# One shared set of fourteen 8 KB buffers in place of separate homes for weights and normed rows

## The chip, the cores and the metric

The kernel runs on one core of a Trainium2 chip. The metric is the device time of one execution in microseconds (us): 773.72 us is the median of three runs (773.42 to 774.41). The core's engines work side by side, each through its own list of instructions in a fixed order: PE (TensorE, matmul), DVE (VectorE), ACT (ScalarE), POOL (GpSimd) and SP (SyncE, which issues the transfers here). Semaphores hold an instruction back until what it needs is there.

## The reference, cut to what matters

```
x: (1, 256, 1024) f32;  for l in range(2):
    sh1,sc1,gt1,sh2,sc2,gt2 = split(silu(c) @ w_ada[l] + b_ada[l], 6)
    h  = rms(x, g_mix[l]) * (1 + sc1) + sh1
    qkv_a, qkv_b(3 groups), gate_a, gate_b = split(h @ w_in[l])
    y_a = gqa_attention(rope(rms(qa)), rope(rms(ka)), va) @ w_branch_a[l]     # 8 query, 2 key/value heads
    y_b = dilated_attention(3 groups x 4 heads) @ w_branch_b[l]
    x  = x + gt1 * ((sigmoid(gate_a)*y_a + sigmoid(gate_b)*y_b) @ w_out[l])
    h2 = rms(x, g_mlp[l]) * (1 + sc2) + sh2
    x  = x + gt2 * (square(relu(h2 @ w_ff1[l])) @ w_ff2[l])                   # hidden width 4096
```

256 rows are two tiles of 128 (t = 0 and 1) on the partitions.

## The kernel before

**Weights.** All weights stream from HBM once, as tiles of 128 x 1024 f32 (512 KB). A tile lands in one of six buffers `wr`, and is split for matmuls in a reduced format: ACT writes the high part (`w<-wr`, a copy that rounds), DVE the low part (`w<-wr,w`, the difference). High and low together are one tile `w2` of 8 KB in each partition. The other operand is split in the same way (`hT`, `mT`, `oa`, `r2k`), and `mm3` makes each product of three matmuls: high by high, low by high, high by low. 236 weight tiles are split so. 96 more (`w_ada`) also land in `wr`, and DVE reduces each against silu(c) in one instruction (`s2k<-wr,c_act`, called an ada below), in the gaps of other work.

**Stages of a layer.** Norm and transposes give `hT` (normed rows, transposed, scaled and shifted; high and low, 8 KB each); then the q, k and v products; attention A (four pairs) and B (two pairs of heads) in pieces between the gate matmuls `g`; the branch products `ya`, `yb`; the output product `wo`; the residual (`s2k<-ps,gtb`, `x<-x,s2k`); then the norm again and the MLP: `ff1` and `ff2`, where a first ff1 tile (f0, four weight tiles) goes by rows t. A norm is a chain over four engines: sum of squares on ACT, `ss` on DVE, a power of one column on POOL (`ss<-ss,half`), two row scalings `xn` on DVE (`s2k<-x,ss`), eight transposes on PE (`ps<-ident,s2k`, called xT), then scale and shift and both parts of `hT` on DVE. The stretches from `wo` to `ff1` and from the MLP of layer 0 to layer 1 are called handoffs below.

**What sets the order.** The program doesn't issue as it is written. `Plan` records every operation, links them by what they read and write (`links`), and lays them out with a model of the engines (`run`, from L330): each engine takes the ready operation with the earliest due time (`due`, L304). Two things there depend on how many buffers a kind of tile has. In `due` (L311 to L325), the users of a tile are due before the first use of the tile that stands as many places later among its kind as there are buffers. In `run`, `fits` (L351 to L363) holds an operation back until a buffer of its kind is free; a tile that starts out of its turn must leave room for those that were written before it. `issue` (L460) then emits the operations in that order. The tiles of kinds in `mixed` (L138, only `"b8"`) share one set of equal buffers, which the tile framework hands out.

**Homes of 8 KB before.** `w2` has four buffers, `hT` two, and `b8` (`NB8`, L40) eight. `b8` holds the attention's q and k tiles, v, `oa`, both gate tiles `G`, the table tile, `M`, both `mT`, and those weight tiles that `spare` marks (patterns `sp_x`, `sp_wo`, `sp_f`, `sp_l` in `CFG`: four of the eight of `wo`, for one). 14 in all.

Of the kernel before, what the change touches and what calls it, by code (L numbers as in the profile page):

```python
# [12 lines left out]
F32R = mybir.dt.float32r  # L13
# [6 lines left out]
P = 128  # L20
D = 1024
S = 256
# [3 lines left out]
KT = D // P  # L26
# [10 lines left out]
  seq0="u c3 w w u c4 w w u a w w w w a v w w w w a w w w w v a w w w w b v w w y y b w w v y y v".split(),  # L37
  seq1="c2 u w w c3 u w w c4 u w w c5 w w a u w w a w w v a w w a v w w b v y y b v y y".split())
WR = 6
NB8 = 8  # L40

# [452 lines left out]
def encoder(ctx: ExitStack, tc: tile.TileContext, a: dict, out: bass.AP):  # L496
# [6 lines left out]
    tl = plan.tile  # L503
# [16 lines left out]
    def f32(t):  # L520
        return t.bitcast(F32)
# [84 lines left out]
    def split_next():  # L606
        src, spare = todo.pop(0)
        i = len(todo)
        raw = tl("sbuf", [P, 1024], F32, "wr", WR, f"wr{i}")
        if spare:  # L610
            w2 = tl("sbuf", [P, 2, 1024], F32R, "b8", NB8, f"w2{i}")
        else:
            w2 = tl("sbuf", [P, 2, 1024], F32R, "w2", 4, f"w2{i}")
        sp.dma_start(raw, src)
        act.activation(w2[:, 0], raw, AF.Copy)
        dve.tensor_tensor(w2[:, 1], raw, f32(w2[:, 0]), op=ALU.subtract)
        ready.append((w2[:, 0], w2[:, 1]))

    def weights(n=None):
        while todo and len(ready) < (n or CFG["ahead"]):  # L620
            split_next()
        return ready.pop(0)
# [37 lines left out]
            yield ps  # L660

    def h_tiles(l, w):
        return [tl("sbuf", [P, KT, S], F32R, "hT", 2, f"hT{l}{w}{i}") for i in range(2)]

    def make_h(l, w, t, hT):
        v = shg[l, w]
# [15 lines left out]
    def rope_tables(l):  # L682
        tabs = tl("sbuf", [P, 2, 2, 8, HD], F32, "b8", NB8, f"tabs{l}")
        for hf in range(2):
            g = s2k(f"gain{l}{hf}")
            sp.dma_start(g, a["gains"][l, hf].partition_broadcast(P))
            gv = g.rearrange("p (s q n) -> p s q n", s=4, q=2)
            act.activation(gv[:, :, 1, :], gv[:, :, 1, :], AF.Copy, scale=8.0)
            g = g.rearrange("p (s n) -> p s n", s=8)
            for t in range(2):  # L690
                for s0, s1, o in ((0, 2, 0), (2, 8, 1)):
                    cs = cst[:, t, o, hf, :]
                    pool.tensor_tensor(
                        tabs[:, t, hf, s0:s1, :], g[:, s0:s1, :],
                        cs[:, None, :].to_broadcast([P, s1 - s0, HD]), op=ALU.mult,
                    )
        return tabs
# [62 lines left out]
    def attention_tiles(l):  # L760
        T = {}

        z = [tl("sbuf", [P, 2, 4, S], F32, "b8", NB8, f"qk{l}{i}") for i in range(2)]
        T["qa"] = z[0][:, 0]
        T["b", 0], T["b", 1], T["b", 2] = z[0][:, 1], z[1][:, 0], z[1][:, 1]
        T["ka"] = tl("sbuf", [P, 1, S], F32, "ka", 1, f"ka{l}")
        v = tl("sbuf", [P, 2, 16, HD], F32, "b8", NB8, f"v{l}")
        T["va"] = [v[:, t, 12:14] for t in range(2)]
        T["vb"] = [v[:, t, 0:12] for t in range(2)]
        oa = tl("sbuf", [P, 2, 4, S], F32R, "b8", NB8, f"oa{l}")  # L770
        T["oa"] = (oa[:, 0], oa[:, 1])
# [172 lines left out]
    def gates(l, hT, G, u, bank):  # L944
        if u % 4 == 0:
            G.append(tl("sbuf", [P, 2048], F32, "b8", NB8, f"G{l}{u}"))
        ps = bank(f"g{l}_{u}")
# [38 lines left out]
    def mixer(l, hT, T):  # L986
# [51 lines left out]
        for t in range(2):  # L1038
            ps = [pb(f"wo{l}_{t}_{c}") for c in range(2)]

            def one(kk, c):
                lh, ll = (z[:, kk, t * P : (t + 1) * P] for z in mT)
                wh, wl = (z[:, c * 512 : (c + 1) * 512] for z in ws[kk])
                mm3(ps[c], lh, ll, wh, wl, kk == 0, kk == KT - 1)

            if t == 0:
                for kk in range(KT):
                    ws.append(weights())
                    for c in range(2):
                        one(kk, c)  # L1050
            else:
                for c in range(2):
                    for kk in range(KT):
                        one(kk, c)
            if t == 0:
                h2 = h_tiles(l, 1)
            with ahead(CFG["hp_norm"]):
                for c in range(2):
                    residual(l, 0, t, c, ps[c])
                    sum_sq(l, 1, t, c)  # L1060
                make_h(l, 1, t, h2)
# [119 lines left out]
    for t in range(2):  # L1181
        for c in range(2):
            sum_sq(0, 0, t, c)
        for g, ps in enumerate(rms_x(0, 0, t)):
            act.activation(
                xT[:, 4 * g : 4 * g + 4, t * P : (t + 1) * P], ps.rearrange("p (k n) -> p k n", k=4), AF.Copy
            )
    hT = h_tiles(0, 0)
    banks = {0: pb, 1: pb, 2: pb, 5: pb} | {c: {"pa": pa, "pt": pt}[z] for c, z in CFG["bk0"].items()}
    pss = {c: [bank(f"q0_{c}_{t}") for t in range(2)] for c, bank in banks.items()}  # L1190
    for k in range(KT):
# [7 lines left out]
        for pair in ((0, 1), (2, 5)):  # L1199
            w = weights(CFG["ahead0"])  # L1200
# [14 lines left out]
    m = mlp(0, h2)  # L1215
    next(m)
    hT = h_tiles(1, 0)
    with ahead(CFG["hp_norm"]):
        make_h(1, 0, 0, hT)
# [108 lines left out]
```

## Time and profile before

| | |
|---|---|
| median of three runs | 773.72 us (773.42 to 774.41) |
| the profiled execution's own time | 775.0 us |
| its span, first to last instruction | 773.2 us |
| busy: PE, weight load, DVE, ACT, POOL | 742.4, 642.0, 588.0, 447.8, 102.9 us |
| share of the chain that ended last: PE, DVE, issue, DMA, ACT | 73%, 15%, 4%, 3%, 3% |
| granted TensorE clock | 1.00 of full speed |
| read from HBM | 179.44 MB, 233 GB/s over the span |

Busy time of PE is modelled at the ends of matmuls, so back-to-back rows overlap a little; the start of one row to the start of the next is the safer measure. The row of an engine ends with the idle time that came before it and what ended it.

### The profile page before, as it was taken

What the parts mean: (1) busy time and instruction counts of PE and PEld (TensorE: products, weight loads), DVE (VectorE), ACT (ScalarE), POOL (GpSimd) and SP (SyncE); (2) the same over time, 40 slices, a digit from 0 to 9 for tenths busy, and PEclk for the clock granted to TensorE, in tenths of its full rate; (3) what the DMA queues carried; (4) which work ended last, traced back from release to release, by engine and by line L of the source; (5) the groups of instructions that cost most, each with busy time, mean ns of one, the idle gap of its engine ahead of it and who ended that gap; (6) DMA issues with size and microseconds to landing.
All of it is one profiled execution on the core that took longest, in us unless ns stands there. A gap on an engine that the chain in (4) does not pass through costs nothing.

```text
span 773.2 us, 12148 instructions
## 1 busy us (share of the span) xinstructions
PE 742.4 (96%) x4632; PEld 642.0 (83%) x4632; DVE 588.0 (76%) x846; ACT 447.8 (58%) x693; POOL 102.9 (13%) x88
## 2 busy tenths in 40 slices
PE   3899999999999999999999999999999999999997
PEld 2677777799778999888878888889976999888896
DVE  5899999877899777885797988966689954545562
ACT  6458557886345555545744555798834654545560
POOL 1306840000000002200013743000000000000000
PEclk9999999999999999999999999999999999999999
DMA  8996678886459989897844576964444976556531
GB/s 338 329 391 216 201 248 277 292 279 212 138 185 371 332 314 320 297 322 253 273 139 133 164 261 231 330 214 137 152 148 136 384 246 191 189 190 191 191 109 54
DMA packets 50666, 181.30 MB, mean 234 GB/s; under 512 B 5648, under 2 KB 5936, under 8 KB 50608
## 3 DMA queue, kind: packets, MB, share of 16 engines
q1 hardware_dynamic: 50608, 180.53, 68.6%
q8 instruction: 36, 0.59, 0.3%
q14 instruction: 22, 0.18, 0.1%
HBM read 179.44 MB, written 1.06 MB: 233 GB/s over the span
## 4 chain that ended last, share of the span: by engine, by line
PE 73%; DVE 15%; issue 4%; DMA 3%; ACT 3%; POOL 1%; SPq 0%; POOLq 0%; DVEq 0%; ACTq 0%
PE ps L492 73%; DVE s2k L492 7%; DVE w L492 4%; DMA ident<-in_ident 1%; DMA wr<-in_w_gate 1%; ACT pr L492 1%; ACT w L492 1%; POOL ss L492 1%; DMA wr<-in_w_ada 1%; ACT s2k L492 1%; DVE rstd L492 1%; DMA wr<-in_w_y 1%; DVE x L492 1%; DVE hT L492 1%; DVE shg L492 0%
## 5 line engine op out<-in xcount | busy, mean ns | idle before, releaser
L492 DVE TENSOR_TENSOR w<-wr,w 128x1024 fp32r<-128x1024 f32 x236 | 291.1, 1244 | 108.9 <-ACT w L492 108.8
L492 ACT ACTIVATE w<-wr 128x1024 fp32r<-128x1024 f32 x236 | 246.9, 1057 | 196.3 <-PE ps L492 161.2
L492 PE MATMUL ps<-hT,w 128*128 128x256 f32 x2112 | 265.1, 282 | 1.0 <-DVE w L492 0.6
L492 PEld LDWEIGHTS ps<-hT,w 128*128 128x128 f32 x2112 | 255.4, 188 | 8.4 <-issue 4.0
L492 PE MATMUL ps<-w,r2k 128*128 128x512 f32 x768 | 181.7, 395 | 0.0
L492 PE MATMUL ps<-w,hT 128*128 128x512 f32 x672 | 166.5, 400 | 6.3 <-DVE w L492 2.6
L492 PEld LDWEIGHTS ps<-w,r2k 128*128 128x128 f32 x768 | 143.1, 188 | 33.1
L492 PEld LDWEIGHTS ps<-w,hT 128*128 128x128 f32 x672 | 123.5, 188 | 39.7 <-ACT hT L492 4.4
L492 DVE CUSTOM_DVE_ANT_0 s2k<-wr,c_act 128x1024 bf16<-128x1024 f32 x96 | 119.1, 1256 | 10.6 <-DMA wr<-in_w_ada 10.5
L492 ACT ACTIVATE s2k<-ps 128x512 f32<-128x512 f32 (+2 forms) x108 | 55.9, 556 | 31.6 <-PE ps L492 30.3
L492 POOL TENSOR_TENSOR ss<-ss,half 128x1 f32<-128x1 f32 x8 | 9.2, 1147 | 307.1 <-DVE ss L492 307.1
L492 POOL TENSOR_TENSOR s2k<-s2k,tabs 128x256 f32<-128x256 f32 (+1 forms) x40 | 37.6, 961 | 87.1 <-ACT s2k L492 37.4
L492 PE MATMUL ps<-w,mT 128*128 128x512 f32 x192 | 45.4, 395 | 0.0
L492 PEld LDWEIGHTS ps<-w,mT 128*128 128x128 f32 x192 | 35.5, 188 | 8.5 <-DVE mT L492 1.2
L492 PE MATMUL ps<-ident,s2k 128*128 128x128 f32 x148 | 23.8, 295 | 16.9 <-DMA ident<-in_ident 11.9
L492 PEld LDWEIGHTS ps<-ident,s2k 128*128 128x128 f32 x148 | 18.0, 149 | 24.0 <-issue 12.7
L492 POOL TENSOR_TENSOR rstd<-rstd,half 128x8 f32<-128x8 f32 (+1 forms) x20 | 36.6, 1844 | 0.2
L492 ACT ACTIVATE pr<-pr,st 128x256 f32<-128x256 f32 (+1 forms) x64 | 35.4, 616 | 1.0 <-DVE st L492 1.0
L492 POOL TENSOR_TENSOR tabs<-s2k,cst 128x384 f32<-128x384 f32 (+1 forms) x16 | 19.9, 1277 | 91.0 <-ACT s2k L492 85.5
L492 DVE TENSOR_TENSOR r2k<-s2k,r2k 128x512 fp32r<-128x512 f32 x28 | 20.4, 729 | 9.6 <-ACT r2k L492 9.4
L492 ACT ACTIVATE s2k<-x 128x512 bf16<-128x512 f32 x16 | 10.0, 625 | 25.0 <-DVE x L492 25.0
L492 ACT ACTIVATE s2k<-s2k 128x512 f32<-128x512 f32 (+1 forms) x36 | 21.9, 609 | 4.3 <-DMA s2k<-in_gains 3.3
(68 smaller groups left out, 463.7 us busy)
## 6 DMA issues: line engine op xcount, KB each, us to landing
wr<-in_w_ff SPq DMA_DIRECT2D x120, 512.0 KB, 4.4
wr<-in_w_ada SPq DMA_DIRECT2D x96, 512.0 KB, 4.6
wr<-in_w_gate SPq DMA_DIRECT2D x32, 512.0 KB, 4.3
wr<-in_w_qkv SPq DMA_DIRECT2D x24, 512.0 KB, 4.3
wr<-in_w_x SPq DMA_DIRECT2D x16, 512.0 KB, 5.6
wr<-in_w_out SPq DMA_DIRECT2D x16, 512.0 KB, 4.3
wr<-in_w_y SPq DMA_DIRECT2D x8, 512.0 KB, 6.1
wr<-in_w_ba SPq DMA_DIRECT2D x8, 512.0 KB, 5.0
```

Of the source, the lines that this page charges most:

```text
L492: getattr(self.real[o["e"]], o["op"])(*map(real, o["a"]), **{n: real(z) for n, z in o["k"].items()})
```

## The change

All tiles of 8 KB come from `b8`, which now has 14 buffers: every `w2`, both `hT`, and what was there already. Memory, instructions and arithmetic stay the same. `spare` no longer selects anything.

```diff
@@ -37,7 +37,7 @@
 WR = 6
-NB8 = 8
+NB8 = 14
...
@@ -607,10 +607,7 @@
         src, spare = todo.pop(0)
         i = len(todo)
         raw = tl("sbuf", [P, 1024], F32, "wr", WR, f"wr{i}")
-        if spare:
-            w2 = tl("sbuf", [P, 2, 1024], F32R, "b8", NB8, f"w2{i}")
-        else:
-            w2 = tl("sbuf", [P, 2, 1024], F32R, "w2", 4, f"w2{i}")
+        w2 = tl("sbuf", [P, 2, 1024], F32R, "b8", NB8, f"w2{i}")
         sp.dma_start(raw, src)
         act.activation(w2[:, 0], raw, AF.Copy)
         dve.tensor_tensor(w2[:, 1], raw, f32(w2[:, 0]), op=ALU.subtract)
@@ -660,7 +657,7 @@
     def h_tiles(l, w):
-        return [tl("sbuf", [P, KT, S], F32R, "hT", 2, f"hT{l}{w}{i}") for i in range(2)]
+        return [tl("sbuf", [P, KT, S], F32R, "b8", NB8, f"hT{l}{w}{i}") for i in range(2)]
```

Since `due` and `fits` go by kinds and their numbers, the order of the instructions moves on every engine. Until the first q products of layer 0 are done it stays as it was; behind that it differs in most places. Three of them are shown. The numbers behind names are buffers; before, `w_0_105` to `w_3_108` are the four `w2` homes, and `hT_94`, `hT_95` the two of `hT`.

**The handoff from wo to ff1 in layer 0, on DVE.** `gtb` rows are the residual, `ISA` with `gcol` is an ada. First the end of `wo` for t = 0; before:

```order
L492 TENSOR_TENSOR w_143<-wr_104,w_143 128x1024
L492 TENSOR_TENSOR s2k_85<-ps_89,gtb_139 128x512
L492 TENSOR_TENSOR x<-x,s2k_85 128x512
L492 TENSOR_TENSOR s2k_84<-ps_91,gtb_139 128x512
L492 TENSOR_TENSOR x<-x,s2k_84 128x512
L492 SCALAR_TENSOR_TENSOR ss_77<-ss_77 128x1
L492 ISA s2k_80,gcol_124<-wr_104,c_act 128x1024
L492 ISA gcol_124 128x1
L492 TENSOR_SCALAR s2k_83<-x,ss_77 128x512
```

And now, where `w_200` and `w_201` are the first two of f0's four weights:

```order
L492 TENSOR_TENSOR w_200<-wr_103,w_200 128x1024
L492 TENSOR_TENSOR w_201<-wr_100,w_201 128x1024
L492 TENSOR_TENSOR s2k_85<-ps_89,gtb_181 128x512
L492 TENSOR_TENSOR x<-x,s2k_85 128x512
L492 TENSOR_TENSOR s2k_83<-ps_91,gtb_181 128x512
L492 TENSOR_TENSOR x<-x,s2k_83 128x512
L492 ISA s2k_80,gcol_142<-wr_104,c_act 128x1024
L492 ISA gcol_142 128x1
L492 SCALAR_TENSOR_TENSOR ss_77<-ss_77 128x1
L492 ISA s2k_81,gcol_142<-wr_100,c_act 128x1024
L492 ISA gcol_142 128x1
L492 TENSOR_SCALAR s2k_84<-x,ss_77 128x512
```

The low parts of these two weights stand ahead of the residual, and one of two adas stands between the residual and `ss`. Next the end of the norm of t = 0 and the residual's second half of t = 1; before, with f0's first three weights in `w_2_107`, `w_3_108` and `w_0_105`:

```order
L492 TENSOR_TENSOR hT_95<-s2k_79,hT_94 128x4x128
L492 TENSOR_TENSOR w_2_107<-wr_102,w_2_107 128x1024
L492 TENSOR_TENSOR s2k_80<-ps_86,gtb_139 128x512
L492 TENSOR_TENSOR x<-x,s2k_80 128x512
L492 TENSOR_TENSOR w_3_108<-wr_100,w_3_108 128x1024
L492 SCALAR_TENSOR_TENSOR ss_78<-ss_78 128x1
L492 TENSOR_TENSOR w_0_105<-wr_101,w_0_105 128x1024
L492 TENSOR_SCALAR s2k_82<-x,ss_78 128x512
```

Now, where `w_202` and `w_203` are f0's third and fourth weight, and `w_204` belongs to the ff1 tile behind it:

```order
L492 TENSOR_TENSOR hT_191<-s2k_80,hT_190 128x4x128
L492 TENSOR_TENSOR w_202<-wr_99,w_202 128x1024
L492 TENSOR_TENSOR s2k_81<-ps_88,gtb_181 128x512
L492 TENSOR_TENSOR x<-x,s2k_81 128x512
L492 TENSOR_TENSOR w_203<-wr_102,w_203 128x1024
L492 SCALAR_TENSOR_TENSOR ss_78<-ss_78 128x1
L492 TENSOR_TENSOR w_204<-wr_101,w_204 128x1024
L492 TENSOR_SCALAR s2k_85<-x,ss_78 128x512
```

The rows have the same kinds in the same order, but other weights: the four of f0 stood here and behind, now the last two do. On PE, all of `wo` for t = 0 now stands ahead of t = 1, the transposes of t = 0 stand behind 22 matmuls of t = 1 (before 21), and those of t = 1 behind 19 matmuls of f0 (before 15). In layer 1 the same rows move; there the counts are 20 (before 21) and 20 (before 15).

**Attention B of layer 0, first pair of heads, on PE.** `ps<-qk` are scores, `ps<-ident,pr` the transposes of what the softmax gives, `w_2_107` before and `w_167` now a weight of gate tile 5 (they count from 0). Before:

```order
L492 MATMUL ps_89<-hT_94,w_2_107 128x256 x2
L492 MATMUL ps_89<-hT_95,w_2_107 128x256
L492 MATMUL ps_87<-qk_110 128x256
L492 MATMUL ps_93<-qk_110 128x256
L492 MATMUL ps_87<-qk_111 128x128
L492 MATMUL ps_93<-qk_111 128x128
L492 MATMUL ps_87<-qk_111 128x128
L492 MATMUL ps_93<-qk_111 128x128
L492 MATMUL ps_88<-ident,pr_134 128x128
L492 MATMUL ps_88<-ident,pr_133 128x128
L492 MATMUL ps_88<-ident,pr_134 128x128
L492 MATMUL ps_88<-ident,pr_133 128x128
```

Now:

```order
L492 MATMUL ps_93<-qk_123 128x128
L492 MATMUL ps_88<-qk_123 128x128
L492 MATMUL ps_92<-qk_122 128x256
L492 MATMUL ps_90<-qk_122 128x256
L492 MATMUL ps_92<-qk_123 128x128
L492 MATMUL ps_90<-qk_123 128x128
L492 MATMUL ps_92<-qk_123 128x128
L492 MATMUL ps_90<-qk_123 128x128
L492 MATMUL ps_87<-ident,pr_157 128x128
L492 MATMUL ps_86<-ident,pr_157 128x128 x2
L492 MATMUL ps_89<-hT_94,w_167 128x256
L492 MATMUL ps_89<-hT_95,w_167 128x256
```

Before, 23 of the 24 matmuls with this gate weight stood ahead of the transposes; now one does, and 23 stand among and behind them. The scores of both halves stand closer together, and the last pair of attention A (written `pr_159`, `pr_160`) stands ahead of them.

**The handoff from the MLP to layer 1, t = 0, on DVE.** Before:

```order
L492 TENSOR_TENSOR s2k_80<-ps_93,gtb_139 128x512
L492 TENSOR_TENSOR x<-x,s2k_80 128x512
L492 TENSOR_TENSOR s2k_84<-ps_89,gtb_139 128x512
L492 TENSOR_TENSOR x<-x,s2k_84 128x512
L492 TENSOR_TENSOR w_165<-wr_102,w_165 128x1024
L492 SCALAR_TENSOR_TENSOR ss_75<-ss_75 128x1
L492 TENSOR_TENSOR w_2_107<-wr_100,w_2_107 128x1024
L492 TENSOR_SCALAR s2k_82<-x,ss_75 128x512
L492 TENSOR_SCALAR s2k_81<-x,ss_75 128x512
```

Now:

```order
L492 TENSOR_TENSOR s2k_83<-ps_90,gtb_181 128x512
L492 TENSOR_TENSOR x<-x,s2k_83 128x512
L492 TENSOR_TENSOR s2k_80<-ps_89,gtb_181 128x512
L492 TENSOR_TENSOR x<-x,s2k_80 128x512
L492 SCALAR_TENSOR_TENSOR ss_75<-ss_75 128x1
L492 TENSOR_SCALAR s2k_82<-x,ss_75 128x512
L492 TENSOR_SCALAR s2k_85<-x,ss_75 128x512
```

The two weight splits between the residual and `xn` are gone from there. On PE the transposes behind this stand 19 matmuls of t = 1 after the end of t = 0, where they stood behind 23.

## Rows read from the trace of the kernel before

**Rows 1.** Busy time by stretch: engines (instructions), clock, DMA share, GB/s

```profile
129.00:160.00 31.00, 29.07 (x247) 24.72 (x246) 26.10 (x56) 25.13 (x54) 0.00 (x0) 1.00 0.83 293
...
226.00:383.00 157.00, 157.00 (x1010) 141.94 (x1009) 122.22 (x145) 89.11 (x110) 11.49 (x8) 1.00 0.88 308
383.00:405.00 22.00, 21.39 (x97) 16.93 (x96) 18.61 (x32) 9.94 (x15) 2.93 (x2) 1.00 0.50 165
```

**Rows 2.** Waits of PE: us in total, times, longest

```profile
PE ps L492 <- DVE s2k L492: 4.7, 9, 1.3
PE ps L492 <- DVE w L492: 3.2, 6, 0.8
```

**Rows 3.** PE in order of time, first handoff: start, us, count, idle before

```profile
206.52 1.09 PE L492 MATMUL ps<-ident,s2k 128*128 128x128 f32 x8 [0.39 <-DVE s2k L492]
...
212.98 0.64 PE L492 MATMUL ps<-w,hT 128*128 128x512 f32 x2
...
214.05 1.66 PE L492 MATMUL ps<-w,hT 128*128 128x512 f32 x6 [0.43 <-DVE w L492]
...
216.52 1.90 PE L492 MATMUL ps<-w,hT 128*128 128x512 f32 x7 [0.81 <-DVE w L492]
...
218.66 1.09 PE L492 MATMUL ps<-ident,s2k 128*128 128x128 f32 x8 [0.25 <-DVE s2k L492]
...
219.51 2.93 PE L492 MATMUL ps<-w,hT 128*128 128x512 f32 x10
...
222.66 1.20 PE L492 MATMUL ps<-w,hT 128*128 128x512 f32 x4 [0.23 <-DVE hT L492]
```

**Rows 4.** PE in layer 1's handoff from wo to ff1

```profile
577.44 5.98 PE L492 MATMUL ps<-w,mT 128*128 128x512 f32 x25
...
583.26 0.64 PE L492 MATMUL ps<-w,hT 128*128 128x512 f32 x2
...
584.45 1.66 PE L492 MATMUL ps<-w,hT 128*128 128x512 f32 x6 [0.55 <-DVE w L492]
```

**Rows 5.** DVE and POOL, norm of t = 0, layer 0's handoff

```profile
204.23 0.16 DVE L492 SCALAR_TENSOR_TENSOR ss<-ss 128x1 f32<-128x1 f32 x1 [0.85 <-ACT s2k L492]
204.31 1.22 DVE L492 CUSTOM_DVE_ANT_0 s2k<-wr,c_act 128x1024 bf16<-128x1024 f32 x1
204.47 1.47 POOL L492 TENSOR_TENSOR ss<-ss,half 128x1 f32<-128x1 f32 x1 [91.46 <-DVE ss L492]
```

**Rows 6.** The same power on POOL in layer 1, t = 0

```profile
575.46 0.56 POOL L492 TENSOR_TENSOR ss<-ss,half 128x1 f32<-128x1 f32 x1 [96.61 <-DVE ss L492]
```

**Rows 7.** PE, second norm of the MLP's handoff

```profile
404.83 1.09 PE L492 MATMUL ps<-ident,s2k 128*128 128x128 f32 x8 [0.54 <-DVE s2k L492]
```

**Rows 8.** PE in attention B of layer 0

```profile
139.67 0.38 PE L492 MATMUL ps<-hT,w 128*128 128x256 f32 x1 [0.40 <-ACT w L492]
140.58 1.15 PE L492 MATMUL ps<-qk 64*128 64x256 f32 x12 [0.53 <-ACT pr L492]
141.88 1.74 PE L492 MATMUL ps<-ident,pr 128*128 128x128 f32 x8 [0.16 <-ACT pr L492]
144.01 0.95 PE L492 MATMUL ps<-hT,w 128*128 128x256 f32 x6 [0.39 <-DVE w L492]
...
149.19 2.00 PE L492 MATMUL ps<-ident,pr 128*128 128x128 f32 x16
...
153.39 0.39 PE L492 MATMUL ps<-hT,w 128*128 128x256 f32 x1
...
154.47 2.98 PE L492 MATMUL ps<-hT,w 128*128 128x256 f32 x23 [0.20 <-DVE w L492]
```

**Rows 9.** ACT in the same stretch, the idle time inside it

```profile
136.48 0.60 ACT L492 ACTIVATE G<-ps 128x512 f32<-128x512 f32 x1 [4.05 <-PE ps L492]
```

**Rows 10.** Chain that ended last, a transfer of that stretch: start, us

```profile
130.91 7.63 DMA wr<-in_w_gate
```

**Rows 11.** PE, the first work of the kernel

```profile
11.89 3.64 PE L492 MATMUL ps<-ident,s2k 128*128 128x128 f32 x16 [11.89 <-DMA ident<-in_ident]
```

## The prediction

> **What bounds the kernel now.** I read the page first, then the busy time by stretch, then who PE waits for, and last the timeline of PE and DVE around those waits. PE bounds the kernel: in the long MLP of layer 0 it is busy for all of 157.00 us [rows 1], so nothing that starts earlier there can shorten it. What can go are the waits inside three kinds of places. By the waits view the largest left after the start are for DVE: 4.7 us for normed rows (`s2k`) and 3.2 us for weights (`w`) [rows 2]; both belong mostly to the handoffs, where DVE has residual, norm, `hT` and weight splits in one queue.
>
> How much PE loses at such a place I take from starts: next start less this start less the count times the spacing of back-to-back matmuls. 25 matmuls of 512 columns between 577.44 and 583.26 give 0.233 each [rows 4].
>
> **Handoff from wo to ff1, layer 0.** Lost before [rows 3]: 0.39 ahead of the transposes of t = 0; 1.07 less two times 0.233 = 0.60 behind the row at 212.98; 2.47 less six times = 1.07 behind 214.05; 2.14 less seven times = 0.51 behind 216.52; 3.15 less ten times = 0.82 behind 219.51. Sum 3.39. The 0.60 and 1.07 are low parts of f0's weights: their four homes were held by `wo` until its end, so the splits fell behind `hT` on DVE, where each costs 1.22.
>
> Now two of the four are split ahead of the residual, where DVE is waiting for PE anyway. That gives PE 12 matmuls, 2.80 us, before it needs the third weight. The third is split right behind `hT`, by about 214.0 (the place of the first one before), needed at 215.8; the fourth by about 216.5, where the second one ended before (the restart at 216.52) [rows 3], needed at 217.2. Both 0.60 and 1.07 go.
>
> What is late next is the norm. For t = 0 an ada has moved ahead of `ss`. DVE idled 0.85 there, and the ada takes 1.22 [rows 5], so the chain comes 0.37 later; PE has one matmul more to cover it (0.23). The wait becomes 0.39 + 0.37 - 0.23 = 0.53. For t = 1 DVE's chain has the same kinds of rows as before, so its transposes can't start before about 218.7 as before, and PE, no longer stopped, gets there after 19 matmuls from 213.1, at 217.5: a wait of 1.2 in place of 0.51. Behind it no split stands between `xn` and `hT`, which takes off up to 0.65, but only 6 matmuls (1.4) in place of 10 cover it: I keep 0.6 of the 0.82. So 0.53 + 1.2 + 0.6 = 2.3, a gain of 1.1. Bounds: 1.7, if the chain of t = 1 comes earlier by 0.6, and 0.2, if a norm takes 0.9 longer.
>
> **The same handoff in layer 1.** Before: 1.19 less two times 0.233 = 0.72 and 2.46 (to the restart that answers to 216.52) less 1.40, about as in layer 0 [rows 4], and the rest as there: 0.72 + 1.07 + 0.51 + 0.82 = 3.1. The transposes of t = 0 didn't wait, because POOL's power took 0.56 [rows 6] where it took 1.47 beside an ada [rows 5]. Now the ada ahead of `ss` costs 0.37, and PE has one matmul less in front: 0.6. With 1.2 and 0.6 as above the sum is 2.4: a gain of 0.7 to 0.8; I take 0.8, with bounds 1.6 and 0.
>
> The row shows what is worth having here: 0.56 with DVE idle, 1.47 with a DVE instruction of 1.22 that began before it. The Trainium skill, "GPSIMD Engine Reference", section "1. Specifications", says that GpSimd's way to SBUF is shared with VectorE and contended by DVE instructions with two SBUF inputs, which an ada is. By that rule layer 0 could keep 1.47, since a second ada stands behind `ss`, and layer 1 could keep 0.56; the sums above come out the same.
>
> **From the MLP to layer 1.** Two splits leave the chain of t = 0. If the power falls from 1.47 to 0.56 the chain is 0.9 shorter; but PE now has 19 matmuls to cover it and not 23, 0.93 less. Net 0. Behind it two splits stand ahead of the residual of t = 1 where one did, yet that residual waits for PE's end; the wait of 0.54 [rows 7] stays. I take 0, with bounds -0.5 and, if the power stays at 1.47, +0.9.
>
> **Attention B of layer 0.** Lost before [rows 8]: 0.40 ahead of the row at 139.67; 0.91 less 0.12 = 0.79 behind it (a matmul of 256 columns is half of 0.233); 2.13 less eight transposes, 0.85 from 218.66 to 219.51 [rows 3], = 1.28 behind 141.88; 1.08 less two matmuls = 0.85 behind 153.39. Sum 3.3. (The idle time by stretch, 31.00 - 29.07 = 1.93 [rows 1], is less, since modelled ends of matmuls cover part.) Meanwhile ACT idled 4.05 [rows 9]. Now the last pair of attention A and its softmax come earlier and fill ACT's gap, and most of those losses go. In their place PE waits at the transposes of the first pair of B. It gets there with 23 matmuls (2.7) less behind it and some 0.8 more of other work, so 1.9 earlier than 149.19, and without 0.40 + 0.79 + 1.28 of losses: at 144.8. The softmax can't gain as much: with ACT's 4.05 filled by some 2 us of other work it is ready around 147.2. A wait of 2.4 (1.0 to 4.2), with 23 gate matmuls queued behind it that can't pass. The 0.85 later goes for the most part, say 0.2 left. 3.3 - 2.6 = a gain of 0.7; bounds 1.8 gained and 0.8 lost.
>
> **Elsewhere.** Until the first q products the order is the same. In 60 to 129 DVE is the busy one and its work is the same; I allow 0.4 either way. MLP: 0, by the full 157.00. Freed homes only let transfers start earlier, and the six `wr` buffers still hold them.
>
> **Sum.** 1.1 + 0.8 + 0 + 0.7 = 2.6. The profiled execution took 775.0 at a span of 773.2, so after the change it would take 772.4; it lay 1.3 above the median of 773.72, and I put the median after at 773.72 - 2.6 = 771.1.
>
> **Rivals.**
> - *All the splits' waits go and nothing follows.* 0.60 + 1.07 twice, 0.7 more of the norms, and 1.8 in attention: 5.0 to 5.8, about 768.5. For it: freed DVE time ahead of the norm. Against it: the chain of t = 1 has the same instructions, and was late already.
> - *The norms eat it.* If the power takes 1.47 at each place, and xT stands where PE gets to it early, the handoffs gain 0.2 and 0, and the MLP's loses 0.9, attention gains 0.7: about 773.5, no change. For it: five of the eight powers took 1.46 or 1.47, as in [rows 5].
> - *Slower: the gate weight of attention B comes late.* Its transfer was issued at 130.91 and took 7.63 [rows 10]; the first gate matmul at 139.67 waited for it through ACT. Three adas now stand ahead of a split that frees its buffer, 3.6 us of DVE work. If the transfer moves by all of it, the scores behind that single matmul, their softmax and the 23 matmuls follow: 3.6 lost, less 0.7 gained, less 1.9 in the handoffs, is 774.7. And PE would idle some 6 us in one piece. The first transposes, after 11.89 of idle PE, took 3.64 for 16, 0.21 each [rows 11], against 1.09 for 8 [rows 3], half the rate: the lower of the two levels, 1.2 GHz. If that came back here, 16 transposes and 23 matmuls at half rate add 1.7 + 2.7, and the time is about 778. [...] The row of the clock is 1.00 through this stretch [rows 1], and nothing so far shows a wait in mid-kernel bringing it down. The Trainium skill, "TensorE: Matmul & The Clock Gate", section "What's actually happening", says that the throttled clock is the default and activity releases it; the start of this trace agrees, and no row here shows a return.
> - *It does nothing*: the shared set is as full as the homes were, since 14 were 14, and splits wait for a buffer as before. Against it: the new order on DVE already has them ahead. 773.7.
>
> **Numbers.** The forecast, 769.9 to 772.3, gets 0.45; all waits gone 0.13; norms eat it 0.26; slower 0.11; nothing 0.05. The measurement tells 0.2% (1.55 us) from no change. Below 772.17 lie the first two and a little of the third: 0.62. Above 775.27 most of the fourth and mishaps that I don't name: 0.11. Between: 0.27. Range 8 in 10: 768.9 to 774.2.
>
> **What would show it.** In the profile after: the waits for `w` fall from 3.2 to under 1.5; those for `s2k` stay above 4; the timeline of PE has a wait of about 1.2 ahead of the transposes of t = 1 in both handoffs; in attention B one wait of 1 to 4 us ahead of 16 transposes, and ACT without its idle 4.05; the MLPs' stretch again without idle PE. The forecast fails if the low parts of f0's third and fourth weight are late again, if the power on POOL is 1.47 in all norms, or if PE's first gate matmul of that tile waits for its transfer by more than 2 us.

## The result and the profile after

The changed kernel takes 769.45 us (median of 4 runs, 768.87 to 770.36), the kernel before beside it 774.07 (773.42 to 775.0): a ratio of 0.9941 [0.9923, 0.9958], 4.6 us less. The forecast was 771.1, with 768.9 to 774.2 for eight times in ten. The profiled execution took 770.36 at a span of 768.6, so its span is 4.6 shorter than that of before, and the two traces show the same difference as the medians. Two executions at a lower granted clock ("after again" at 1169.71 us and 0.58, the kernel before in another batch at 912.3 us and 0.76) are left out of the medians below.

Who PE waits for, now (us in total, times, longest):

```profile
PE ps L492 <- DVE s2k L492: 7.2, 10, 1.8
PE ps L492 <- ACT hT L492: 3.6, 5, 1.2
PE ps L492 <- ACT pr L492: 1.9, 2, 1.0
PE ps L492 <- DVE hT L492: 1.6, 3, 0.7
PE ps L492 <- DVE w L492: 0.5, 2, 0.3
```

The waits for weights fell from 3.2 to 0.5, those for normed rows rose from 4.7 to 7.2 [rows 2]: by this view alone little would be won. Busy time of the three stretches of [rows 1]:

```profile
129.00:160.00 31.00, 29.97 (x264) 26.54 (x263) 28.63 (x60) 28.62 (x59) 0.00 (x0) 1.00 0.87 309
226.00:383.00 157.00, 157.00 (x1009) 143.19 (x1008) 117.09 (x142) 87.40 (x108) 12.08 (x8) 1.00 0.84 312
383.00:405.00 22.00, 21.02 (x100) 17.06 (x99) 19.51 (x37) 8.93 (x14) 2.02 (x2) 1.00 0.31 97
```

In attention PE idles 1.03 in place of 1.93; the MLP is as full as before; around the MLP's handoff PE idles more (0.98 for 0.61). The granted clock is 1.00 in all three.

The difference by stage, from the start of the first matmul of one stage to that of the next, in us. "Lost" is the part of it by which gaps between starts exceed those of back-to-back matmuls.

| stage | before | after | difference | lost, before to after |
|---|---|---|---|---|
| start and q, k, v of layer 0 (same order) | 64.88 | 65.20 | +0.3 | 6.2 to 7.4 |
| attention, layer 0 | 118.53 | 116.67 | -1.9 | 19.1 to 17.3 |
| ya/yb, wo, handoff and f0, layer 0 | 56.98 | 55.37 | -1.6 | 4.1 to 3.0 |
| MLP of layer 0 | 151.86 | 150.62 | -1.2 | 0.4 to 0.2 |
| handoff to layer 1, its q, k, v | 43.02 | 44.53 | +1.5 | 1.2 to 2.6 |
| attention, layer 1 | 118.91 | 119.71 | +0.8 | 11.1 to 11.6 |
| ya/yb, wo, handoff and f0, layer 1 | 56.57 | 54.60 | -2.0 | 3.8 to 2.2 |
| MLP of layer 1 and the end | 162.45 | 161.9 | -0.6 | 0.4 to 0.1 |

The MLP of layer 0 had almost nothing to lose and is 1.2 shorter: its matmuls themselves follow each other faster. That was in no step of the prediction. (In a row `ps<-a,b`, a is the moving operand, whose columns run through PE, and b the stationary one, which a weight load brings in first.) The two shapes that make it up, in the MLP of layer 1 (PE's timeline: start, us, count), before:

```profile
679.62 10.43 PE L492 MATMUL ps<-w,r2k 128*128 128x512 f32 x44
689.89 11.47 PE L492 MATMUL ps<-hT,w 128*128 128x256 f32 x96
701.19 3.20 PE L492 MATMUL ps<-w,r2k 128*128 128x512 f32 x13
```

and after:

```profile
679.79 5.65 PE L492 MATMUL ps<-w,r2k 128*128 128x512 f32 x24
685.28 11.68 PE L492 MATMUL ps<-hT,w 128*128 128x256 f32 x96
696.80 7.50 PE L492 MATMUL ps<-w,r2k 128*128 128x512 f32 x32
```

From start to start, 44 matmuls of 512 columns took 10.27 before (233 ns each), 24 take 5.49 now (229). But 96 of 256 columns took 11.30 (117.7) and now 11.52 (120.0). The same instructions on the same shapes, with no wait among them, run at other distances, one kind faster and one slower. Over the whole trace, back-to-back distance times count, for all matmuls on split weights: 662.1 before, 659.9 now. The start shows what can become of such a gain: its order is the same, its 512-column matmuls follow faster, but 1.2 more is lost in waits and the stage is no shorter.

### The profile page after: what moved, and what is told of

Its sections match the earlier page's. It is cut to its first block, busy times and chain, and to the rows that moved or that the text cites. A ratio compares the mean times of both kernels' runs of the same rounds, so it can differ in the third digit from the quotient of the medians.

```text
span 768.6 us, 12113 instructions
## 1 busy us (share of the span) xinstructions
PE 736.4 (96%) x4632; PEld 646.9 (84%) x4632; DVE 583.3 (76%) x846; ACT 445.4 (58%) x693; POOL 104.4 (14%) x88
## 4 chain that ended last, share of the span: by engine, by line
PE 70%; DVE 19%; issue 5%; DMA 2%; ACT 2%; POOL 1%; SPq 0%; POOLq 0%; DVEq 0%
PE ps L492 70%; DVE s2k L492 10%; DVE w L492 6%; DMA ident<-in_ident 1%; DVE rstd L492 1%; DMA wr<-in_w_ada 1%; DVE hT L492 1%; ACT pr L492 1%; POOL ss L492 1%; DVE x L492 1%; DMA wr<-in_w_gate 1%; ACT w L492 1%; DVE st L492 0%; ACT s2k L492 0%; SPq L492 0%
## 5 line engine op out<-in xcount | busy, mean ns | idle before, releaser
L492 PE MATMUL ps<-hT,w 128*128 128x256 f32 x2112 | 270.4, 285 | 0.3 <-DVE w L492 0.3
L492 PEld LDWEIGHTS ps<-hT,w 128*128 128x128 f32 x2112 | 260.1, 191 | 7.0 <-issue 3.6
L492 PE MATMUL ps<-w,r2k 128*128 128x512 f32 x768 | 178.7, 392 | 0.0
L492 PE MATMUL ps<-w,hT 128*128 128x512 f32 x672 | 162.1, 395 | 5.4 <-ACT hT L492 3.6
L492 DVE CUSTOM_DVE_ANT_0 s2k<-wr,c_act 128x1024 bf16<-128x1024 f32 x96 | 118.7, 1254 | 7.8 <-DMA wr<-in_w_ada 7.5
L492 POOL TENSOR_TENSOR s2k<-s2k,tabs 128x256 f32<-128x256 f32 (+1 forms) x40 | 39.5, 1009 | 84.7 <-DVE w L492 36.3
L492 DVE TENSOR_TENSOR s2k<-ps,gtb 128x512 f32<-128x512 f32 x16 | 11.0, 686 | 24.3 <-PE ps L492 24.3
```

Of the source, the lines that this page charges most:

```text
L492: getattr(self.real[o["e"]], o["op"])(*map(real, o["a"]), **{n: real(z) for n, z in o["k"].items()})
```

## The experiments

The kernel before was timed beside each batch (774.4 to 774.9), and "time" is the difference to it. "Spacing" is the sum just named, against before; it is counted from the trace of each kernel, and good to some 0.3.

| kernel | median, us | ratio [95%] | time | spacing |
|---|---|---|---|---|
| before, 64 B moved | 774.79 | 1.0002 [0.9992, 1.0012] | +0.1 | 0 |
| after, 64 B moved | 770.38 | 0.9951 [0.9939, 0.9964] | -4.3 | -2.2 |
| weights alone shared | 771.57 | 0.9968 [0.9957, 0.998] | -3.1 | +0.2 |
| hT alone shared | 771.65 | 0.996 [0.9948, 0.9972] | -3.2 | -6.0 |
| weights shared, hT 64 B on | 766.46 | 0.9902 [0.9885, 0.992] | -8.2 | -9.3 |
| before's order, after's spacing | 774.98 | 1.0004 [0.9995, 1.0013] | +0.1 | -1.1 |
| before's order, placed | 769.46 | 0.9935 [0.9921, 0.9949] | -5.4 | -8.0 |
| after again | 769.42 | 0.9937 [0.9924, 0.9951] | -5.0 | -2.2 |
| after's order, placed | 764.54 | 0.9875 [0.986, 0.9889] | -9.9 | -9.2 |

**Does the address itself matter?** First idea: the start of an operand modulo 128 sets the distance. A constant of 64 B is put ahead of all buffers, in the kernel after and in the kernel before:

```diff
...
-    half = cp.tile([P, 16], F32, name="half")
+    half = cp.tile([P, 32], F32, name="half")
...
```

> The changed kernel with the constant tile half widened from 16 to 32 columns, so that every buffer behind it in SBUF starts 64 bytes later; no instruction moves on any engine. Placement theory: the start to start spacing of matmuls goes by where the operands start modulo 128 bytes. In the changed kernel weights and hT start at 64, r2k at 0; 512-column matmuls with the weight as moving operand take 0.228 to 0.229 us each there, against 0.233 before, where the moving weight starts at 0. Here weights and hT start at 0 and r2k at 64, so the 512-column ones should be back at 0.233 (1631 of them, some 4 to 5 ns each: 6 to 8 us), the 256-column ones stay at 0.120: about 776 to 777 us. Order theory (the whole gain is in the order of the instructions and the waits it removes): as the changed kernel, 769.5 us.

> The kernel before with the same widened tile; no instruction moves. The four weight homes now start at 64 modulo 128 bytes (before at 0), hT and the shared eight at 0 (before at 64), r2k at 64. Placement theory: 512-column matmuls fall from 0.233 to about 0.229 (some 1440 of them with a weight from the four homes: 5 to 6 us), 256-column ones stay at 0.118 (weight and hT still in different halves): 768 to 770 us, as fast as the changed kernel without its order. Order theory: as before, 774 us.

770.38 and 774.79: neither kernel moves, and the distances stay. The first theory falls. What a common shift leaves alone is the difference between the starts of a matmul's two operands. Sorted by that difference (moving operand less stationary one, modulo 256 B), the distances of all kernels fall together:

| difference, B | 256 columns, ns | 512 columns, ns |
|---|---|---|
| 0 | 119.8 to 119.9 | 226.9 to 229.3 |
| 64 | 117.8 to 117.9 | 229.0 to 230.5 |
| 128 | 118.7 to 119.4 | 231.5 to 233.2 |
| 192 | 115.6 to 117.8 | 232.8 to 233.4 |

(means over a pair of operands, such as `hT` and weights, in one kernel; at 192 the 256-column ones ran at 117.8 in some stretches and at 114 in others, at 128 at 120.0 and at 118.5, and what decides between these is open. 42 matmuls of 512 columns, few enough to leave out, took 231.6 at 0.) The change moves `hT` less weights from 64 to 0 and, for most of them, weights less `hT` from 192 to 0 and weights less `r2k` from 128 to 64: 2112 times 2.0 ns lost, 672 times 5.2 and 768 times 3.9 won. With the small groups that is 2.2 us won.

**One half of the change at a time.** Only the weights from the shared set (12 buffers), `hT` in its two homes; and only `hT` (10 buffers):

```diff
-NB8 = 8
+NB8 = 12
...
-        if spare:
-            w2 = tl("sbuf", [P, 2, 1024], F32R, "b8", NB8, f"w2{i}")
-        else:
-            w2 = tl("sbuf", [P, 2, 1024], F32R, "w2", 4, f"w2{i}")
+        w2 = tl("sbuf", [P, 2, 1024], F32R, "b8", NB8, f"w2{i}")
```

> Only the weights join the shared set (12 buffers); hT keeps its two homes. The order on DVE at the handoffs from wo to ff1 is that of the changed kernel, and so are the starts modulo 128 (weights 64, hT 64). If the weights' sharing makes the gain: as the changed kernel, 768.5 to 770.5 us, with the waits of PE for w at 0.5 us or less. If hT's sharing has a part: between that and 774.

```diff
-NB8 = 8
+NB8 = 10
...
-        return [tl("sbuf", [P, KT, S], F32R, "hT", 2, f"hT{l}{w}{i}") for i in range(2)]
+        return [tl("sbuf", [P, KT, S], F32R, "b8", NB8, f"hT{l}{w}{i}") for i in range(2)]
```

> Only hT joins the shared set (10 buffers); the weights keep their four homes and the eight shared ones by spare. The order on DVE at the handoffs from wo to ff1 is that of before (two of f0's splits behind hT of t = 0), and operand starts keep their differences modulo 256 bytes. If the weights' sharing makes the gain: as before, within 1 us of it. If hT's sharing has a part: 1 to 3 us under before.

The two come out alike, 771.57 and 771.65, by different ways. The first is above the 768.5 to 770.5 that was expected if the weights made the whole gain: `hT` less weights went to 128, where its matmuls are slow in both shapes. For the second it was expected that the starts keep their differences, and they don't: `hT` less weights goes from 64 to 192. PE's waits for `w` are no longer among its largest with the weights alone, and with `hT` alone they are larger than before:

```profile
PE ps L492 <- DVE w L492: 4.0, 6, 0.9
PE ps L492 <- ACT hT L492: 1.8, 3, 1.0
```

That is the second kernel (from its longest execution, 773.43), its order at the handoffs about that of before. Its gain stands where its spacing fell by 6.0, of which about half did not arrive in the time. The first has no gain in spacing (+0.2) and is 3.1 faster: a gain by the order of the weights alone, which is the prediction's mechanism.

**Spacing against order.** In the kernel with shared weights 64 unused bytes were put ahead of `hT`; the order stays the same on every engine:

```diff
...
+        if not pad:
+            pad.append(plan.pools["sbuf"].tile([P, 16], F32, name="pad", tag="pad", bufs=1))
         return [tl("sbuf", [P, KT, S], F32R, "hT", 2, f"hT{l}{w}{i}") for i in range(2)]
```

> The same with 64 unused bytes ahead of hT's homes: the order of the instructions stays as in the run with the weights alone shared, but hT now starts at 0 modulo 128 while the weights stay at 64; r2k goes to 64. Placement theory: 256-column matmuls (2112 with hT moving, weight stationary) fall from 0.120 to 0.118, 4 us; 512-column ones stay near 0.228 to 0.230 since the moving weight stays at 64: 765 to 766.5 us. Order theory: as the run without the pad.

766.46, 5.1 less than without them: 64 bytes that nobody reads are worth more than the whole change was. Next the kernel before, in its order, with such pads ahead of `w2` and `ka`: of 64 bytes to give most pairs the differences of after, then of 128.

```diff
...
+            pad("w2")
             w2 = tl("sbuf", [P, 2, 1024], F32R, "w2", 4, f"w2{i}")
...
+        pad("ka")
         T["ka"] = tl("sbuf", [P, 1, S], F32, "ka", 1, f"ka{l}")
```

> The order of before, with 64 unused bytes ahead of the four weight homes and 64 ahead of the key tile, so that a weight's start less hT's is 0 modulo 256 bytes, and less r2k's is 64, as in the changed kernel (before: 192 and 128). Placement theory, in the form that the four runs left (the difference of the two operands' starts modulo 256 counts, not the start of one): 256-column matmuls of hT rise from 117.8 to 119.8 ns (1995 of them, +4.0 us), 512-column ones fall from 233.1 to 227.9 and from 233.4 to 229 (some 600 and 700 of them, -3.1 and -3.1 us), the rest +0.3: 1.9 us under before. What then is missing to the changed kernel, 2.7 us, would be the order's. Order theory: as before.

> The kernel before, every instruction in its order and every buffer in its fixed home, with 128 unused bytes ahead of the homes of w2 and ahead of ka. That alters nothing but the starts of tiles: modulo 256 bytes, hT minus the weights 192 (before 64), the weights minus hT 64 (192), the weights minus r2k 0 and for a few 64 (128 and 64). Theory of the spacing by the difference of the two starts: 2112 matmuls of 256 columns 117.8 to 116.8 ns (-2 us), 672 of 512 on hT 233.4 to 229.5 (-2.6), 768 of 512 on r2k 233 to 227 (-4.6): some 8 to 9 us less work, of which some comes back as waits; 766 to 769.5 us. Theory of the order of work (placement does nothing by itself): as before, 774 to 775.

The first doesn't move (774.98), where 1.9 us less was expected. Only half of after's 2.2 of spacing was reproduced, since spare weights got other differences, and that half did not arrive: PE's waits for `s2k` went from 4.7 to 5.2, those for `hT` from ACT from 2.3 to 2.8. The second goes to 769.46, to the edge of what was expected: 8.0 of spacing, 5.4 of time (waits for `s2k`: 7.1). Last the kernel after, in its order, with buffers 8448 B apart, `hT` and `oa` 192 B into theirs and 64 B behind the set:

```diff
...
-            z = self.pools[pool].tile(shape, dt, tag=tag, bufs=bufs, name=name)
-            t = Tile(f"{name}_{len(self.tiles)}", tag, shape, dt, z)
+            z = self.pools[pool].tile([P, 2048 + 64], F32, tag=tag, bufs=bufs, name=name)
+            at = 48 if name[:2] in ("hT", "oa") else 0
+            t = Tile(f"{name}_{len(self.tiles)}", tag, shape, dt)
+            z = t.own = t.base(z[:, at : at + 2048])
...
```

> The changed kernel with the same order on every engine, where only addresses differ: shared buffers 8448 bytes apart, hT and oa 192 bytes into theirs, 64 unused bytes behind the set. The first operand's start less the second's, modulo 256, becomes 192 for hT and oa as moving operands of 256 columns (now 0), 64 for weights against hT (now 0) and 0 for weights against r2k (now 64). Placement theory, with the spacings that the runs so far showed for these differences: 2112 + 192 matmuls fall from 119.8 to 116.8 ns (-6.9 us), 672 rise from 228 to 229.5 (+1.0), 768 fall from 229 to 227 (-1.5): 7.4 us less work for PE; where DVE or the transfers set the pace the time comes back as waits, some 2 to 3.5 us: 4 to 5.5 us under the changed kernel. Order theory: as the changed kernel.

PE's timeline of this kernel, the same shapes as above:

```profile
679.75 11.47 PE L494 MATMUL ps<-hT,w 128*128 128x256 f32 x96
691.05 11.04 PE L494 MATMUL ps<-w,r2k 128*128 128x512 f32 x48
701.93 2.28 PE L494 MATMUL ps<-hT,w 128*128 128x256 f32 x18
```

117.7 and (10.88 / 48) 226.7 ns: both better than after's. 764.54, and so order and placement add up. Taken from the column "time", the order is worth 5.1 at the first placement (+0.1 less -5.0) and 4.5 at the second (-5.4 less -9.9). The two kernels of a pair still differ by 1.1 and 1.2 of spacing; if all of that arrives, 4.0 and 3.3 are left. Directly, the change's 4.6 less all its 2.2 of spacing is 2.4. So the order is worth between 2.4 and 5.1, by the two matched pairs at least 3.3 and 4.0. Of the spacing that came with the change at most its 2.2 arrived, by these two figures 0.6 to 1.3.

**POOL's power.** Each norm's `ss` goes through one instruction on POOL. Its rows in the kernel after (layer 0, t = 0; layer 1's first norm, t = 0 and 1; layer 1's second, t = 0):

```profile
202.00 1.47 POOL L492 TENSOR_TENSOR ss<-ss,half 128x1 f32<-128x1 f32 x1 [88.13 <-DVE ss L492]
...
386.74 0.55 POOL L492 TENSOR_TENSOR ss<-ss,half 128x1 f32<-128x1 f32 x1 [86.80 <-DVE ss L492]
399.54 1.46 POOL L492 TENSOR_TENSOR ss<-ss,half 128x1 f32<-128x1 f32 x1 [12.25 <-DVE ss L492]
...
572.23 0.56 POOL L492 TENSOR_TENSOR ss<-ss,half 128x1 f32<-128x1 f32 x1 [95.17 <-DVE ss L492]
```

In the two of 1.46 and 1.47 an ada or a split had begun on DVE, at 201.84 and 399.38 here; both powers end 0.4 after it does. In the two of 0.55 and 0.56 DVE ran nothing beside them.

```profile
200.63 1.22 DVE L492 CUSTOM_DVE_ANT_0 s2k<-wr,c_act 128x1024 bf16<-128x1024 f32 x1
...
201.77 0.15 DVE L492 SCALAR_TENSOR_TENSOR ss<-ss 128x1 f32<-128x1 f32 x1
201.84 1.22 DVE L492 CUSTOM_DVE_ANT_0 s2k<-wr,c_act 128x1024 bf16<-128x1024 f32 x1
...
203.51 0.88 DVE L492 TENSOR_SCALAR s2k<-x,ss 128x512 f32<-128x512 f32 x2 [0.44 <-POOL ss L492]
...
399.38 1.22 DVE L492 TENSOR_TENSOR w<-wr,w 128x1024 fp32r<-128x1024 f32 x1
```

To test it, one ada and three splits that stand between `ss` and `xn` are put behind `xn`, with the transfers that wait for their buffers; nothing else moves:

```diff
...
+        ss = [j for j in pw["need"] if self.ops[j]["op"] == "scalar_tensor_tensor"]
+        xn = [j for j, _ in pw["next"] if self.ops[j]["op"] == "tensor_scalar"]
...
+            if o["e"] == "DVE" and split(o) and not any(z["e"] == "PE" and tiles(z) & tiles(o) for z in part):
+                later.append(o)
...
+        order[k : end + 1] = stay + later
```

> The changed kernel with four DVE instructions of 1.22 us (one ada, three weight splits), which stand between ss and xn, put behind xn, in both handoffs from wo to ff1 and for t = 1 of the handoff from the MLP; their transfers' successors move with them. Lock theory (POOL's power of one column waits while a DVE instruction of two SBUF operands runs): the power falls from 1.47 to 0.56 in these four places, PE's waits ahead of the transposes (0.46, 1.12 and what answers to them in the other two) shrink by up to 0.9 each, and since the moved instruction then delays hT by 0.3 to 0.6, 1.5 to 2 us are gained in all: 767.5 to 768.5. Rival (the power takes 1.47 for another reason, as the engine waking up): it stays at 1.47, and the time at 769.5 to 770.5.

The same power as at 202.00, and DVE around it:

```profile
200.50 0.56 POOL L516 TENSOR_TENSOR ss<-ss,half 128x1 f32<-128x1 f32 x1 [87.70 <-DVE ss L516]
```

```profile
200.27 0.16 DVE L516 SCALAR_TENSOR_TENSOR ss<-ss 128x1 f32<-128x1 f32 x1
201.09 0.88 DVE L516 TENSOR_SCALAR s2k<-x,ss 128x512 f32<-128x512 f32 x2 [0.67 <-POOL ss L516]
201.89 1.22 DVE L516 CUSTOM_DVE_ANT_0 s2k<-wr,c_act 128x1024 bf16<-128x1024 f32 x1
```

All six of these powers take 0.55 or 0.56, and `xn` starts 0.82 after `ss` where it took 1.74 (203.51 less 201.77). 768.29 us, a ratio of 0.9913 [0.9899, 0.9926]: 1.1 below the 769.42 of after (1.9 by the ratios, 0.9937 less 0.9913, since they were timed in different batches). The Trainium skill, "SBUF — State Buffer", section "Who interferes with whom", has the rule: a DVE instruction with two inputs in SBUF contends with a GpSimd instruction that reads there, and the port pair that the two engines share is an exclusive lock; these rows agree (0.56 alone, 1.47 beside one). What a DVE instruction with one input there would do, no run here shows. The same edit on the kernel with shared weights and 64 B, after once more as the measure, and the edit on the placed kernel:

> The kernel with the weights alone shared and the pad ahead of hT (766.5 us), with the same moves as in the run with the norm first. If the two effects are independent: 1.5 to 2 us under it, 764.5 to 765 us. If with faster matmuls PE waits for DVE in more places, less: 765.5 to 766.5.

> The changed kernel as it is, on the chip of the next two, for comparison: 4 to 5 us under before (ratio 0.9941).

> The same with the four DVE instructions behind xn, as in the run of the changed kernel with the norm first. If the effects add up: 1 to 2 us under the run with the addresses alone, 762 to 764.5 us where before takes 774.5. If the faster matmuls only reach the next wait for DVE: within 0.7 us of it.

765.3 (0.9876 [0.9862, 0.9889]), 1.2 less than without (2.0 by the ratios); 769.42, as the first time; and 762.69 (0.9853 [0.9838, 0.9868]), 1.8 less than without. The last is the fastest of all, 6.7 below the changed kernel.

## Why the prediction was right, and where it wasn't

The time lies inside the range, 0.55 from its lower end, and below the 769.9 to 772.3 of the forecast proper. Its mechanism, the order of f0's splits, did what was said. That the sum came as near as it did is in part luck: several terms were off by 1 to 2 us, to both sides, and one was missing.

**Handoff from wo to ff1, layer 0: right, term by term.** PE now:

```profile
204.05 1.09 PE L492 MATMUL ps<-ident,s2k 128*128 128x128 f32 x8 [0.46 <-DVE s2k L492]
204.90 6.18 PE L492 MATMUL ps<-w,mT 128*128 128x512 f32 x26
210.92 4.47 PE L492 MATMUL ps<-w,hT 128*128 128x512 f32 x19
216.51 1.09 PE L492 MATMUL ps<-ident,s2k 128*128 128x128 f32 x8 [1.12 <-DVE s2k L492]
217.36 1.40 PE L492 MATMUL ps<-w,hT 128*128 128x512 f32 x5
219.09 0.50 PE L492 MATMUL ps<-w,hT 128*128 128x512 f32 x1 [0.32 <-DVE hT L492]
```

f0's 19 matmuls run without a stop, where [rows 3] had two. Left are 0.46 (said: 0.53; the ada put `ss` off by 0.21, from 1.54 to 1.75 behind the start of the last residual row, and not by 0.37), 5.59 less 19 times 0.228 = 1.26 (1.2), and 1.73 less five times = 0.59 (0.6). Sum 2.3, gain 1.1, as forecast. The stage is 1.6 shorter; the rest is mostly spacing.

**The same in layer 1: right mechanism, too small.**

```profile
573.36 1.09 PE L492 MATMUL ps<-ident,s2k 128*128 128x128 f32 x8
...
580.67 4.70 PE L492 MATMUL ps<-w,hT 128*128 128x512 f32 x20
585.94 1.09 PE L492 MATMUL ps<-ident,s2k 128*128 128x128 f32 x8 [0.58 <-DVE s2k L492]
586.79 1.17 PE L492 MATMUL ps<-w,hT 128*128 128x512 f32 x4
588.52 0.51 PE L492 MATMUL ps<-w,hT 128*128 128x512 f32 x1 [0.56 <-DVE hT L492]
```

The term of 0.6 ahead of the first transposes is zero: the row at 573.36 shows no wait. It was 0.37 for the ada and 0.23 for a matmul less in front. The ada put `ss` off by 0.22 only, and the count was wrong: before, 19 matmuls of t = 1 and not 21 stood between the last one of t = 0, which starts at 571.89 in that trace, and the transposes at 576.59. Now 20 do (568.45 to 573.36), so there is a matmul more in front, and the two cancel. The power at 572.23 stayed at 0.56. At t = 1, 5.27 less 20 times 0.228 = 0.71 in place of 1.2, then 0.82 in place of 0.6. So 1.5 is lost, not 2.4: a gain of 1.6, the bound that the prediction gave, where it took 0.8.

**From the MLP to layer 1: wrong.** The prediction took 0; 1.4 more is lost. The power of t = 0 did fall to 0.55, but the wait at t = 1 grew:

```profile
395.45 5.15 PE L492 MATMUL ps<-w,hT 128*128 128x512 f32 x22
401.58 1.09 PE L492 MATMUL ps<-ident,s2k 128*128 128x128 f32 x8 [0.98 <-DVE s2k L492]
...
416.88 10.91 PE L492 MATMUL ps<-w,hT 128*128 128x512 f32 x47
428.58 0.66 PE L492 MATMUL ps<-ident,s2k 128*128 128x128 f32 x4 [0.80 <-DVE s2k L492]
```

The step that failed is "that residual waits for PE's end". DVE's part of it:

```profile
393.25 2.35 DVE L492 TENSOR_TENSOR w<-wr,w 128x1024 fp32r<-128x1024 f32 x2
395.52 0.68 DVE L492 TENSOR_TENSOR s2k<-ps,gtb 128x512 f32<-128x512 f32 x1
```

And before, DVE and the same row of PE:

```profile
397.63 1.22 DVE L492 TENSOR_TENSOR w<-wr,w 128x1024 fp32r<-128x1024 f32 x1
398.77 0.68 DVE L492 TENSOR_TENSOR s2k<-ps,gtb 128x512 f32<-128x512 f32 x1
...
399.01 5.28 PE L492 MATMUL ps<-w,hT 128*128 128x512 f32 x22
```

The residual starts as the second split ends, with no idle time between them: it waited for DVE. It did so before too, behind its one split, so these rows already spoke against that step. Its chain came 0.31 later against PE's row of 22 than before (395.52 to 395.45; before 398.77 to 399.01). Those 22 matmuls are also 0.11 quicker now, so PE comes earlier to a chain that DVE paces. The wait of 0.80 at 428.58, ahead of a q tile's transposes, is new too; 0.98 is lost there. The prediction hadn't looked that far behind the handoff. On DVE three splits in a row stand ahead of this chain's end:

```profile
422.89 4.18 DVE L492 TENSOR_TENSOR w<-wr,w 128x1024 fp32r<-128x1024 f32 x3
```

Before there were two (2.89 at 426.07). That the third makes the wait is likely, but no run took it away.

**Attention B of layer 0: direction right, too small.**

```profile
142.43 2.02 PE L492 MATMUL ps<-qk 64*128 64x256 f32 x24
145.48 0.55 PE L492 MATMUL ps<-ident,pr 128*128 128x128 f32 x3 [1.03 <-ACT pr L492]
...
151.46 3.73 PE L492 MATMUL ps<-hT,w 128*128 128x256 f32 x29
155.03 5.20 PE L492 MATMUL ps<-oa,w 128*128 128x256 f32 x42
```

The one wait at the transposes stands where it was put, at 144.5 (144.8 was said), but takes 1.03, the lower bound, not 2.4. The softmax was ready at 145.4, not 147.2: ACT's idle 4.05 is gone, and the longest gap left in that stretch is

```profile
137.46 1.06 ACT L492 ACTIVATE w<-wr 128x1024 fp32r<-128x1024 f32 x1 [1.31 <-DMA wr<-in_w_gate]
```

The stage loses 1.8 less, the bound again (by the prediction's own terms, 3.3 less 0.2 and less 1.0 or 4.2, the bounds were 2.1 gained and 1.1 lost). No experiment isolated attention's part.

**Elsewhere.** "The same spacing" was never said; it was assumed, in every sum. That is the missed term, 2.2 of spacing (of which about 1 may have arrived), and it is what the MLPs' 0 missed (-1.2, -0.6). Attention of layer 1, +0.8, was in no step either.

**Rivals.** *Slower* didn't come: the gate weight of B reached ACT at 137.46 after a wait of 1.31, PE's first matmul with it (142.11) shows no idle time, and the clock is 1.00. (With the half rate its terms add up to 779.1, not 778.) *Nothing* is out by the order's 2.4 or more. *The norms eat it* was half there, four powers of six at 1.46 to 1.48 and the wait behind the MLP longer; moving four instructions freed 1.1 to 1.9. *All the waits go* is nearer in time (768.5, off by 1.0) and not in the way: waits for `s2k` rose. The time lay 1.65 below the forecast. Layer 1's handoff and attention gave some 1.9 more, the gaps in the MLPs 0.5 and spacing 2.2; the handoff behind the MLP, layer 1's attention and the start took back 1.4, 0.5 and 1.2 in waits. Together that is 1.5.

## What to carry to other kernels

Sharing buffers among kinds of tiles acted here mostly through the order that it allows: read which operation goes ahead of the chain that PE waits for next, and how far that chain reaches. It also moves addresses: compare the back-to-back distance of each matmul shape in both traces before putting a difference down to waits, and try pads of 64 and 128 bytes once. Keep DVE free of instructions with two SBUF inputs while a small GpSimd instruction stands in a chain that PE waits for.

## What was not expected of the hardware

The distance of back-to-back matmuls on f32 split tiles followed the difference of the two operands' starts modulo 256 B, as far as multiples of 64 B were tried: 115.6 to 119.9 ns at 256 columns and 226.9 to 233.4 at 512, and the best difference isn't the same for the two (0 is the best at 512 columns and the worst at 256). A shift of both by 64 B changed nothing. The kernels that differ from another in the placement of tiles alone (771.57 and 766.46, 774.8 and 769.46, 769.42 and 764.54) show that it is the placement; why the chip does so, no run here tells. And spacing won doesn't arrive whole: 8.0 gave 5.4 in the order of before, and PE's waits for `s2k` rose from 4.7 to 7.1: it then comes sooner to chains that DVE paces.
